# Attention probabilities transposed in 32x32 blocks and put in place by DMAs, instead of by TensorE

## The chip, the cores and the metric

The kernel runs on one core of a Trainium2 chip. The metric is the device time of one execution in microseconds; a kernel's time is the median of its runs.

## The reference

Two post-norm encoder layers over 512 tokens of width 1024, in float32. Each layer projects its input once for three kinds of attention: a (4 heads, dilated windows, written here as one dense softmax with an additive mask), b (8 query heads on 2 key heads, dense) and c (4 heads, a 2-D neighbourhood with a learned bias). Each is projected back to 1024, weighted by a sigmoid gate, and summed; then an output projection, a layer norm, a squared-ReLU MLP and another layer norm.

```
for layer in range(DEPTH):
    h = x @ w_in[layer]
    qa, ka, va, qb, kb, vb, qc, kc, vc, gate_logits = jnp.split(h, splits, axis=-1)
    ...
    merged = (g[:, :, 0] * (oa @ w_branch_a[layer])
              + g[:, :, 1] * (ob @ w_branch_b[layer])
              + g[:, :, 2] * (oc @ w_branch_c[layer]))
    mix = merged @ w_out[layer]
    x = layer_norm(DEEPNORM_ALPHA * x + mix, ln1_g[layer], ln1_b[layer])
    ff = jnp.square(jax.nn.relu(x @ w_up[layer])) @ w_down[layer]
    x = layer_norm(DEEPNORM_ALPHA * x + ff, ln2_g[layer], ln2_b[layer])
```

## The kernel before

Every large product is made of three matmuls: each operand is split into a high part (`whi`, `xTh`, `pth`; ScalarE rounds to fp32r) and a low part (`wlo`, `xTl`, `ptl`; VectorE subtracts), and hi x hi, lo x hi and hi x lo are summed in PSUM. Weights of 512 KB stream through two `raw` buffers (L194, issued by SyncE) and are split at L182 (ScalarE) and L183 (VectorE).

Attention goes over 64 slots a layer: heads a0 to a3, c0 to c3, b0 to b7, each in four blocks of 128 queries (`qb`). A slot's scores `pss` (two matmuls, L513 and L514) are made two slots ahead; then the maximum (L519 in b, L523 in a and c), its negative (L524), the exponential with its sum (L525), the reciprocal (L528) and the normalise (L529: GpSimd in a and b, VectorE in c). `turn` transposes p on TensorE, 128 keys at a time (L544, tile `psp`), and splits the result from PSUM into `pth` and `ptl`. When the head's four blocks are there, `values` multiplies them with the values (`pso`, L558 and L559, eight matmuls), one slot into the next head; ScalarE and VectorE bring the result together in `of` (L568, L569), and after each second head it is split into `oh` and `ol`.

Between the slots a queue of other work fills TensorE: projections, gates (`psg`, L585 is their tanh) and branch projections (`psb`, L607). `rate` says how many matmul triples of this filler go with each half of a slot. L617 is a GpSimd addition that merges a gated branch into `mg`. What each engine does stands in one fixed order of its own, which the compiler's scheduler chooses from the program's order. After the last head, `tail` computes the gates and branches of b, and the MLP follows.

## Time and profile before

| | before |
|---|---|
| median of 3 runs | 1547.91 us |
| lowest to highest | 1545.48 to 1548.38 us |
| the profiled execution | 1549.4 us |
| its span | 1547.6 us |
| TensorE busy (matmul) | 1527.6 us, 99% |
| VectorE busy | 866.0 us, 56% |
| ScalarE busy | 632.5 us, 41% |
| GpSimd busy | 182.0 us, 12% |

The span runs from the first to the last instruction of the profiled execution; 1.8 us of its own time lie around it. Shares are of the span, so they average over stages that differ.

### The profile page before, as it was taken

What the parts mean: (1) busy time and instruction counts of PE and PEld (TensorE: products, weight loads), DVE (VectorE), ACT (ScalarE), POOL (GpSimd) and SP (SyncE); (2) the same over time, 40 slices, a digit from 0 to 9 for tenths busy, and PEclk for the clock granted to TensorE, in tenths of its full rate; (3) what the DMA queues carried; (4) which work ended last, traced back from release to release, by engine and by line L of the source; (5) the groups of instructions that cost most, each with busy time, mean ns of one, the idle gap of its engine ahead of it and who ended that gap; (6) DMA issues with size and microseconds to landing.
All of it is one profiled execution on the core that took longest, in us unless ns stands there. A gap on an engine that the chain in (4) does not pass through costs nothing.

```text
span 1547.6 us, 19148 instructions
## 1 busy us (share of the span) xinstructions
PE 1527.6 (99%) x7400; PEld 1279.8 (83%) x7400; DVE 866.0 (56%) x1498; ACT 632.5 (41%) x1036; POOL 182.0 (12%) x190
## 2 busy tenths in 40 slices
PE   8999999999999999999999999999999999999997
PEld 6888888888898888888888888888888888888886
DVE  4678877644664314441566787776448542244315
ACT  4665666533144212431136556665332431134310
POOL 0113213211100000000102141233111000000001
PEclk9999999999999999999999999999999999999999
DMA  6222311153153323332331323112432432233311
GB/s 218 83 85 75 111 55 58 52 177 123 55 177 96 96 82 96 110 96 83 106 128 56 98 82 103 55 59 95 146 123 83 136 99 92 82 123 95 96 55 55
DMA packets 43434, 150.61 MB, mean 97 GB/s; under 512 B 5072, under 2 KB 5712, under 8 KB 43344
## 3 DMA queue, kind: packets, MB, share of 16 engines
q1 hardware_dynamic: 43344, 149.40, 30.5%
q8 instruction: 58, 0.95, 0.2%
q14 instruction: 32, 0.26, 0.1%
HBM read 145.19 MB, written 4.19 MB: 97 GB/s over the span
## 4 chain that ended last, share of the span: by engine, by line
PE 95%; DVE 2%; ACT 1%; DMA 1%; issue 0%; POOL 0%; SPq 0%; POOLq 0%; DVEq 0%; ACTq 0%
PE psd L155 9%; PE psd L154 9%; PE psd L153 9%; PE psu L154 8%; PE psu L155 8%; PE psu L153 8%; PE psg L155 6%; PE psg L154 6%; PE psg L153 6%; PE psp L544 3%; PE psq L155 2%; PE psq L153 2%; PE psq L154 2%; PE psb L155 2%; PE psb L153 2%; PE psb L154 2%
## 5 line engine op out<-in xcount | busy, mean ns | idle before, releaser
L183 DVE TENSOR_TENSOR wlo<-raw,whi 128x1024 fp32r<-128x1024 f32 (+1 forms) x246 | 306.9, 1248 | 421.5 <-ACT whi L182 420.5
L182 ACT ACTIVATE whi<-raw 128x1024 fp32r<-128x1024 f32 (+1 forms) x246 | 258.4, 1053 | 462.8 <-PE psd L155 143.1
L153 PE MATMUL psu<-xTh,whi 128*128 128x512 f32 (+1 forms) x576 | 210.8, 366 | 0.0
L154 PE MATMUL psu<-xTl,whi 128*128 128x512 f32 (+1 forms) x576 | 210.7, 366 | 0.0
L155 PE MATMUL psu<-xTh,wlo 128*128 128x512 f32 (+1 forms) x576 | 210.5, 365 | 0.0
L153 PE MATMUL psd<-whi,hh 128*128 128x512 f32 x512 | 199.3, 389 | 0.0
L155 PE MATMUL psd<-whi,hl 128*128 128x512 f32 x512 | 199.2, 389 | 0.0
L154 PE MATMUL psd<-wlo,hh 128*128 128x512 f32 x512 | 199.2, 389 | 0.0
L153 PE MATMUL psg<-xTh,whi 128*128 128x512 f32 x384 | 156.8, 408 | 0.0
L154 PE MATMUL psg<-xTl,whi 128*128 128x512 f32 x384 | 151.6, 395 | 0.0
L155 PE MATMUL psg<-xTh,wlo 128*128 128x512 f32 x384 | 151.6, 395 | 0.0
L154 PEld LDWEIGHTS psu<-xTl,whi 128*128 128x128 f32 x576 | 108.6, 189 | 17.7
L153 PEld LDWEIGHTS psu<-xTh,whi 128*128 128x128 f32 x576 | 108.6, 189 | 17.4
L155 PEld LDWEIGHTS psu<-xTh,wlo 128*128 128x128 f32 x576 | 108.6, 189 | 17.4
L266 POOL TENSOR_TENSOR ve<-ve,nhalf 128x1 f32<-128x1 f32 x16 | 24.2, 1513 | 775.0 <-DVE ve L265 775.0
L529 POOL TENSOR_SCALAR p<-p,stat 128x512 f32<-128x512 f32 x96 | 70.7, 737 | 360.2 <-DVE stat L528 242.9
L154 PEld LDWEIGHTS psd<-wlo,hh 128*128 128x128 f32 x512 | 96.1, 188 | 20.0
L153 PEld LDWEIGHTS psd<-whi,hh 128*128 128x128 f32 x512 | 96.1, 188 | 19.9
L155 PEld LDWEIGHTS psd<-whi,hl 128*128 128x128 f32 x512 | 96.1, 188 | 19.8
L153 PE MATMUL psq<-whi,xTh 128*128 128x512 f32 (+1 forms) x256 | 90.0, 351 | 7.2 <-ACT whi L182 6.7
L229 DVE TENSOR_TENSOR ptl<-psp,pth 128x512 fp32r<-128x512 f32 (+2 forms) x128 | 81.6, 637 | 21.2 <-ACT pth L228 19.8
L155 PE MATMUL psq<-whi,xTl 128*128 128x512 f32 (+1 forms) x256 | 87.9, 343 | 0.0
(116 smaller groups left out, 2572.7 us busy)
## 6 DMA issues: line engine op xcount, KB each, us to landing
raw<-in_w_up SPq DMA_DIRECT2D x64, 512.0 KB, 3.6
raw<-in_w_down SPq DMA_DIRECT2D x64, 512.0 KB, 3.5
raw<-in_w_gate SPq DMA_DIRECT2D x48, 512.0 KB, 3.5
raw<-in_w_qkv SPq DMA_DIRECT2D x22, 512.0 KB, 3.6
raw<-in_w_out SPq DMA_DIRECT2D x16, 512.0 KB, 3.6
raw<-in_w_c SPq DMA_DIRECT2D x12, 512.0 KB, 3.5
bias<-in_rpb SPq DMA_DIRECT2D x8, 640.0 KB, 3.9
raw<-in_w_bb SPq DMA_DIRECT2D x8, 512.0 KB, 3.6
```

Source lines behind the costliest of these rows:

```text
L153: nc.tensor.matmul(ps, lhs.hi, rhs.hi, start=start, stop=False)
L154: nc.tensor.matmul(ps, lhs.hi, rhs.lo, start=False, stop=False)
L155: nc.tensor.matmul(ps, lhs.lo, rhs.hi, start=False, stop=stop)
L182: nc.scalar.activation(hi[:, s], raw[:, s], AF.Copy)
L183: nc.vector.tensor_tensor(lo[:, s], raw[:, s], f32(hi[:, s]), op=ALU.subtract)
L229: nc.vector.tensor_tensor(dst.lo, ps, f32(dst.hi), op=ALU.subtract)
L266: nc.gpsimd.tensor_tensor(ve[:, 1:], ve[:, :1], nhalf[:, :1], op=ALU.pow)
L529: (nc.vector if name == "c" else nc.gpsimd).tensor_scalar(p, p, st[:, 3:4], 1.0, op0=ALU.mult, op1=ALU.mult)
L544: nc.tensor.transpose(ps[:, j * P:(j + 1) * P], p[:, j * P:(j + 1) * P], ident)
```

## The change

Each block of p is transposed by one VectorE instruction in 32x32 blocks (L552 of the new kernel) into `tx` (three buffers). When a head's four blocks are done, 16 DMAs of 32 rows by 2 KB (`gather`, L562; SyncE's queue, for the last head ScalarE's as well) put the blocks in place in `ptl` (two buffers). `settle` copies each quarter of it, rounded, to `pth`, which takes over the head's `tx` buffer (ScalarE, L577), and subtracts (GpSimd, L578). The values products of a head (L592) come two heads later instead of one. c's normalise moves from VectorE to GpSimd, and the blocks that c's neighbourhood never uses are zeroed by GpSimd. The maximum comes negated, so that L524 goes. `p` has three buffers instead of four, weights have 4 + 4 buffers instead of 5 + 3, the filler rates of c and b fall, and the tail makes half a gate ahead (`half_gate`).

```diff
-            pool, n = (extra[0], 3) if more else (wts, 5)
+            pool = extra[0] if more else wts
-            hi = pool.tile([P, 1024], F32R, tag="whi", name="whi", bufs=n)
-            lo = pool.tile([P, 1024], F32R, tag="wlo", name="wlo", bufs=n)
+            hi = pool.tile([P, 1024], F32R, tag="whi", name="whi", bufs=AHEAD)
+            lo = pool.tile([P, 1024], F32R, tag="wlo", name="wlo", bufs=AHEAD)
...
-            p = pool.tile([P, S], F32, tag="p", name="p", bufs=4)[:, :n]
+            p = pool.tile([P, S], F32, tag="p", name="p", bufs=3)[:, :n]
...
-                (nc.vector if name == "c" else nc.gpsimd).tensor_scalar(p, p, st[:, 3:4], 1.0, op0=ALU.mult, op1=ALU.mult)
+                nc.gpsimd.tensor_scalar(p, p, st[:, 3:4], 1.0, op0=ALU.mult, op1=ALU.mult)
...
-            ps = bank("psp")[:, :n * P]
-            for j in range(n):
-                nc.tensor.transpose(ps[:, j * P:(j + 1) * P], p[:, j * P:(j + 1) * P], ident)
-            split_psum(pt[:, k0:k1, qb * P:(qb + 1) * P], ps.rearrange("p (k q) -> p k q", q=P))
+            nc.vector.transpose(squares[name, h][1][:, :, k0:k1, qb].rearrange("p j k b -> p k j b"),
+                                p.rearrange("p (k j a) -> p k j a", j=4, a=SQ))
+
+        def gather(name, h, queues):
+
+            n, sq = squares[name, h]
+            lo = pool.tile([P, 4, TB, P], F32R, tag=f"ptl{n % 2}", name="ptl", bufs=1)
+            parts[name, h] = Split(None, lo)
+            for m in range(16):
+                i, j = m % 4, m // 4
+                queues[m % len(queues)].dma_start(f32(lo)[j * SQ:(j + 1) * SQ, i],
+                                                  sq[i * SQ:(i + 1) * SQ, j].rearrange("a k q b -> a k (q b)"))
...
+        def settle(name, h, kbs, engines=(nc.gpsimd, nc.gpsimd)):
+
+            pt = parts[name, h]
+            if pt.hi is None:
+                pt.hi = pool.tile([P, 4, TB, P], F32R, tag=f"tx{squares[name, h][0] % 3}", name="pth", bufs=1)
+            for kb in kbs:
+                q = keys_of(name, kb)
+                hi, lo = chosen(pt.hi[:, :, kb], *q), chosen(pt.lo[:, :, kb], *q)
+                nc.scalar.activation(hi, f32(lo), AF.Copy)
+                engines[kb % 2].tensor_tensor(lo, f32(lo), f32(hi), op=ALU.subtract)
...
-        rate = {"a": 2.1, "c": 2.85, "b": 1.6}
+        rate = {"a": 2.1, "c": 2.75, "b": 1.5}
...
-            if qb == 0 and i:
-                values(*slots[i - 1][:2])
-                if (name, h) == ("a", 2):
-                    flags.add("a")
             turn(name, h, qb, probs.popleft())
+            if qb == TB - 1:
+                gather(name, h, (nc.sync,) if i < len(slots) - 1 else (nc.sync, nc.scalar))
+                if i > TB:
+                    settle(*slots[i - TB][:2], (0, 1))
+            if qb in (0, 1) and i >= 2 * TB:
+                at = slots[i - 2 * TB][:2]
+                if qb == 0:
+                    settle(*at, (2, 3))
+                else:
+                    values(*at)
+                    if at == ("a", 1):
+                        flags.add("a")
...
         def tail():
-            steps = 0
+            a, b = slots[-1 - TB][:2], slots[-1][:2]
+            settle(*a, (2, 3))
+            ts = [drain(half_gate("b", 0))]
+            values(*a)
+            settle(*b, range(TB), (nc.vector, nc.gpsimd))
+            ts.append(drain(half_gate("b", 1)))
+            values(*b)
             for m in range(KB):
-                for _ in gated("b", m):
-                    steps += 1
-                    if steps == 4:
-                        values(*slots[-1][:2])
+                drain(gated("b", m, ts[m]))
+                if m + 2 < KB:
+                    ts.append(drain(half_gate("b", m + 2)))
                 yield merged[m]
```

The order of the instructions shows where this puts them. TensorE before, in the first layer, just ahead of the values products of head b1 (the next eight rows): psp_2418 is the last transposed block of b1, pss_2428 the scores of a later slot, psb_2437 six branch matmuls.

```order
L544 MATMUL psp_2418<-ident_73,p_2343 128x128 x4
L153 MATMUL psg_2369<-xTh_80,whi_2330 128x512
L154 MATMUL psg_2369<-xTl_81,whi_2330 128x512
L155 MATMUL psg_2369<-xTh_80,wlo_2331 128x512
L513 MATMUL pss_2428<-kh_1797,qs_2184 128x512
L514 MATMUL pss_2428<-kl_1798,qs_2184 128x512
L153 MATMUL psb_2437<-oh_1639,whi_2238 128x512
L154 MATMUL psb_2437<-ol_1640,whi_2238 128x512
L155 MATMUL psb_2437<-oh_1639,wlo_2239 128x512
L153 MATMUL psb_2437<-oh_2023,whi_2238 128x512
L154 MATMUL psb_2437<-ol_2024,whi_2238 128x512
L155 MATMUL psb_2437<-oh_2023,wlo_2239 128x512
```

TensorE of the change around the values products of head b1 (pso_2449): pss_2428 is now the last scores of head b3, psb_2442 six branch matmuls.

```order
L515 MATMUL pss_2428<-kh_1810,qs_2139 128x512
L516 MATMUL pss_2428<-kl_1811,qs_2139 128x512
L156 MATMUL psb_2442<-oh_1872,whi_2339 128x512
L157 MATMUL psb_2442<-ol_1873,whi_2339 128x512
L158 MATMUL psb_2442<-oh_1872,wlo_2340 128x512
L156 MATMUL psb_2442<-oh_2184,whi_2339 128x512
L157 MATMUL psb_2442<-ol_2185,whi_2339 128x512
L158 MATMUL psb_2442<-oh_2184,wlo_2340 128x512
L592 MATMUL pso_2449<-pth_2382,v_669 128x512
L592 MATMUL pso_2449<-ptl_2232,v_669 128x512
L592 MATMUL pso_2449<-pth_2382,v_669 128x512
L592 MATMUL pso_2449<-ptl_2232,v_669 128x512
```

The psp rows are gone, and the products of b1 (four of the eight shown) stand six matmuls behind the last scores of b3. GpSimd of the change at the same place: L532 is the normalise (p_2327, p_2355, p_2396 and p_2431 are the four blocks of b3, p_2431 made from pss_2428), ptl_2083 and ptl_2232 belong to b0 and b1, mg_487 is a merge.

```order
L578 TENSOR_TENSOR ptl_2083<-ptl_2083,pth_2249 128x4x128 x4
L532 TENSOR_SCALAR p_2327<-p_2327,stat_2328 128x512
L532 TENSOR_SCALAR p_2355<-p_2355,stat_2356 128x512
L532 TENSOR_SCALAR p_2396<-p_2396,stat_2397 128x512
L532 TENSOR_SCALAR p_2431<-p_2431,stat_2432 128x512
L661 TENSOR_TENSOR mg_487<-mg_487,t_2258 128x512
L578 TENSOR_TENSOR ptl_2232<-ptl_2232,pth_2382 128x4x128 x4
L532 TENSOR_SCALAR p_2483<-p_2483,stat_2484 128x512
```

GpSimd had only normalises and merges here; now a head's four subtractions stand together behind all four normalises of the head two later. ScalarE of the change at the start of the tail: t_3015 is the tanh of the second gate, pth_3044 and pth_3142 are the heads b6 and b7, whi_3092 the weights of the next gate.

```order
L231 ACTIVATE oh_2997<-of_2866 128x512
L562 DMA ptl_3027<-tx_2961 32x512 x6
L624 ACTIVATE t_3015<-psg_3016,hb_293 128x512
L577 ACTIVATE pth_3044<-ptl_2921 128x4x128 x4
L577 ACTIVATE pth_3142<-ptl_3027 128x4x128 x4
L185 ACTIVATE whi_3092<-raw_3088 128x1024
L185 ACTIVATE whi_3096<-raw_3090 128x1024
```

The eight pth copies stand ahead of the weights; on TensorE twelve branch matmuls follow the gate psg_3016, and then the gate that needs whi_3092.

## Rows read from the trace of the kernel before

**Rows 1.** The page: busy time by engine, and the granted clock in 40 slices.

```profile
PE 1527.6 (99%) x7400; PEld 1279.8 (83%) x7400; DVE 866.0 (56%) x1498; ACT 632.5 (41%) x1036; POOL 182.0 (12%) x190
...
PEclk9999999999999999999999999999999999999999
```

**Rows 2.** Busy time by window: five b heads, then the four c heads (layer one).

```profile
core 0: us, PE busy (x) PEld busy (x) DVE busy (x) ACT busy (x) POOL busy (x), PEclk, DMA share, GB/s
218.80:291.45 72.65, 72.65 (x361) 59.81 (x360) 53.47 (x108) 44.40 (x88) 22.87 (x26) 1.00 0.19 59
...
115.50:192.30 76.80, 76.80 (x383) 64.38 (x382) 64.46 (x158) 46.38 (x92) 21.87 (x21) 1.00 0.29 91
```

**Rows 3.** Groups by line and shape: TensorE's transposes (busy us, mean ns, idle before).

```profile
L544 PE MATMUL psp<-ident,p 128*128 128x128 f32 x464 | 72.0, 274 | 4.6 <-POOL p L529 4.6
```

**Rows 4.** Timeline of TensorE around one group of transposes (start us, us).

```profile
223.42 0.39 PE L155 MATMUL psg<-xTh,wlo 128*128 128x512 f32 x1
223.65 0.60 PE L544 MATMUL psp<-ident,p 128*128 128x128 f32 x4
224.00 0.48 PE L153 MATMUL psg<-xTh,whi 128*128 128x512 f32 x1
224.32 0.40 PE L154 MATMUL psg<-xTl,whi 128*128 128x512 f32 x1
```

**Rows 5.** Timeline of TensorE at the first transpose of layer one.

```profile
50.41 0.39 PE L153 MATMUL psg<-xTh,whi 128*128 128x512 f32 x1
53.08 0.66 PE L544 MATMUL psp<-ident,p 128*128 128x128 f32 x4 [2.28 <-POOL p L529]
```

**Rows 6.** Busy time by window, just behind the first transposes of layer one.

```profile
53.79:57.20 3.41, 3.41 (x9) 2.67 (x8) 1.64 (x5) 1.40 (x3) 0.57 (x1) 0.50 0.37 141
```

**Rows 7.** Groups by line and shape: the operations that the sum is made of.

```profile
L519 DVE TENSOR_REDUCE stat<-pss 128x1 f32<-128x512 f32 x64 | 43.8, 685 | 3.7 <-PE pss L514 3.3
L528 DVE RECIPROCAL stat<-stat 128x1 f32<-128x1 f32 x128 | 20.5, 160 | 44.8 <-ACT p L525 43.9
L229 DVE TENSOR_TENSOR ptl<-psp,pth 128x512 fp32r<-128x512 f32 x96 | 66.1, 689 | 20.4 <-ACT pth L228 19.5
L183 DVE TENSOR_TENSOR wlo<-raw,whi 128x1024 fp32r<-128x1024 f32 x242 | 304.2, 1257 | 420.3 <-ACT whi L182 419.3
L529 DVE TENSOR_SCALAR p<-p,stat 128x384 f32<-128x384 f32 x16 | 7.9, 491 | 0.2
...
L525 ACT ACTIVATE p<-pss,stat 128x512 f32<-128x512 f32 x64 | 44.0, 687 | 51.1 <-DVE stat L524 50.8
L525 ACT ACTIVATION_READ_ACCUMULATOR p<-pss,stat 128x1 f32 x64 | 12.4, 194 | 0.0
L228 ACT ACTIVATE hh<-r 128x512 fp32r<-128x512 f32 x64 | 40.4, 631 | 77.4 <-DVE r L844 77.4
L585 ACT ACTIVATE t<-psg,hb 128x512 f32<-128x512 f32 x32 | 21.7, 677 | 0.0
L182 ACT ACTIVATE whi<-raw 128x1024 fp32r<-128x1024 f32 x242 | 255.8, 1060 | 461.4 <-PE psd L155 143.1 <-DMA raw<-in_w_up 88.7 <-PE psu L154 87.6
...
L529 POOL TENSOR_SCALAR p<-p,stat 128x512 f32<-128x512 f32 x96 | 70.7, 737 | 360.2 <-DVE stat L528 242.9 <-DVE stat L524 90.9 <-PE pss L514 8.2
L617 POOL TENSOR_TENSOR mg<-mg,t 128x512 f32<-128x512 f32 x32 | 43.8, 1369 | 158.6 <-DVE t L607 158.6
```

**Rows 8.** Timelines of VectorE and GpSimd where they meet in SBUF.

```profile
345.49 2.35 DVE L183 TENSOR_TENSOR wlo<-raw,whi 128x1024 fp32r<-128x1024 f32 x1
...
345.46 1.29 POOL L617 TENSOR_TENSOR mg<-mg,t 128x512 f32<-128x512 f32 x1 [6.96 <-DVE t L607]
...
310.85 2.20 POOL L617 TENSOR_TENSOR mg<-mg,t 128x512 f32<-128x512 f32 x1 [4.23 <-DVE t L607]
```

**Rows 9.** SyncE's timeline (four issues), and the page's DMA issues (KB, us to landing).

```profile
1.64 1.85 SPq L194 DMA_DIRECT2D raw<-in_w_qkv  x4
...
raw<-in_w_gate SPq DMA_DIRECT2D x48, 512.0 KB, 3.5
```

More of the change, by code (lines that the diff above doesn't have):

```diff
@@ L29 @@
 RAWS = 2
+AHEAD = 4
+FIRST = [1, 1, 0, 0, 0, 0]
+SQ = 32
 NEG = -1e30
@@ L327, in project @@
                     yield cost
+                if tb == TB - 1:
+                    stream.free(w[i])
                 if i == nw - 1:
-                    if tb == TB - 1:
-                        for c in w:
-                            stream.free(c)
                     evac(tb, ps[tb])
@@ L418, in c_values @@
         def c_values(m):
-            while m == 0 and "a" not in flags:
+            while m == 0 and "a" not in flags or m == 1 and ("a", 1) not in oT:
                 yield None
@@ L536, in turn @@
             if qb == 0:
[L537 to L545 removed]
+                n = len(squares)
@@ L556, in values @@
                 q0, q1 = keys_of(name, kb)
-                sl = slice(q0 * P, q1 * P)
-                nc.tensor.matmul(po[:, sl], v[:, kb], pt.hi[:, kb, sl], start=i == 0, stop=False, skip_group_check=True)
-                nc.tensor.matmul(po[:, sl], v[:, kb], pt.lo[:, kb, sl], start=False, stop=i == TB - 1, skip_group_check=True)
+                to = chosen(po.rearrange("p (i r) -> p i r", i=4), q0, q1)
+                for n, part in enumerate((pt.hi, pt.lo)):
+                    nc.tensor.matmul(to, v[:, kb], chosen(part[:, :, kb], q0, q1), start=(i, n) == (0, 0),
+                                     stop=(i, n) == (TB - 1, 1), skip_group_check=True)
             half = (h % 2) * HD
@@ L565, in values @@
             if name == "c":
-                dst = by_columns(dst)
-                a, b = blocks(a), blocks(b)
-            nc.scalar.activation(dst, a, AF.Copy)
-            nc.vector.tensor_tensor(dst, dst, b, op=ALU.add)
+                to = dst.rearrange("p (i r q c) -> p i r q c", i=4, r=2, q=TB)
+                cut = [(lambda t, r=r: t.rearrange("p (i q r c) -> p i r q c", i=4, q=TB, r=2)[:, :, r], to[:, :, r])
+                       for r in range(2)]
+            else:
+                cut = [(lambda t: t.rearrange("p (i q b) -> p i q b", i=4, q=TB), dst.rearrange("p (q i b) -> p i q b", q=TB, i=4))]
+            for f, to in cut:
+                nc.scalar.activation(to, f(a), AF.Copy)
+                nc.vector.tensor_tensor(to, to, f(b), op=ALU.add)
             if half:
@@ L619, in branch_c @@
         def branch_c():
-            for m in range(KB):
-                yield from gated("c", m)
+            ts = []
+            for m in range(KB + 1):
+                if m < KB:
+                    ts.append((yield from half_gate("c", m)))
+                if m:
+                    while ("c", 1) not in oT:
+                        yield None
+                    yield from gated("c", m - 1, ts[m - 1])
         g = lambda br, ms: [w_gate[l, br * KB + m] for m in ms]
@@ L765, in encoder @@
     xp = right.enter_context(tc.tile_pool(name="x", bufs=1, side="right", reuse_waits="tile"))
-    stream.plan([w_qkv[0, i] for i in range(6)])
+    extra[0] = right.enter_context(tc.tile_pool(name="early", bufs=1, side="right", reuse_waits="tile"))
+    stream.plan([w_qkv[0, i] for i in range(6)], FIRST)
     def split_x(tb, t, cut):
```

57 lines of the change are left out of this document (37 added, 20 removed).

## Prediction

> **What bounds the kernel now.** I read the page's totals first. TensorE is busy 1527.6 of 1547.6 us, 99%, and its clock is at nine tenths or more in every slice [rows 1]; so what TensorE no longer does is gained, and what makes it wait is lost, one for one. Then the stretches: in a window of five b heads TensorE is busy for all 72.65 us, VectorE 53.47 (74%), ScalarE 44.40 (61%), GpSimd 22.87 (31%) [rows 2]. A b head takes 14.5 us there (72.65/5), and the other engines have slack. The reader should keep both shares in mind: the change gives TensorE less and GpSimd, the slowest engine for one operation, more. Last I read the one place in attention where TensorE already waits, the start of each layer's heads [rows 5, 6], since it shows what a wait does to the clock.
>
> All sums are made against the profiled execution's own 1549.4 us (span 1547.6 and 1.8 around it), 0.1% above the median of 1547.91. The three runs spread over 0.2%, so a difference under 0.2% (3 us) can't be told from none.
>
> **What goes.** The 464 transposes of p on TensorE go [rows 3]: 128 groups, 64 a layer (16 in a; 8 of three and 8 of two in c; 32 in b). Their busy time of 72.0 us is not their price, since matmuls overlap. The starts of neighbours show it: matmuls follow each other by 0.23 us (223.42 to 223.65), and from the start of the four transposes to the second matmul behind them 0.67 us pass (223.65 to 224.32) [rows 4], so a group of four costs 0.67 - 0.23 = 0.44 us, and in proportion three 0.33 and two 0.22. A layer has 48 x 0.44 + 8 x 0.33 + 8 x 0.22 = 25.5 us, both 51.0 us. In b the lower rate (1.5 for 1.6) also takes fillers out of the heads; the fillers left over (about 36 matmuls) run behind the last head, at no loss of their own.
>
> At the first transpose of a layer TensorE waits 2.28 us for p from GpSimd [rows 5], and the next 3.4 us run at a granted clock of 0.50, the 1.2 GHz level [rows 6]. No transpose stands there any more. I count 2.3 + 1.7 (half of 3.4) = 4 a layer, 8 us. Gains: 59 us, to 1490.4 if nothing else moved.
>
> **What is added off the path.** VectorE: 128 block transposes in place of 128 subtractions ptl of 0.69 us. The trace has no such operation. Below, the normalise of 384 elements at 0.49 gives 0.65 for 512 by size, and if it were twice as quick per element 0.33; above, the subtraction of twice the size takes 1.257 [rows 7]. I take 0.69, as nearly all VectorE rows of 512 elements do, so the swap is free; VectorE had 26% idle. ScalarE: pth is read from SBUF instead of PSUM, 0.631 by the row of hh, which reads SBUF too. SyncE: 16 transfers a head, 0.46 us of issue each (1.85/4), 7.4 us, and a 512 KB load lands 3.5 us after issue [rows 9]; some 11 us after the last transpose of head h all should be there, while settling starts only behind the last normalise of head h+2, two head times (over 25 us) on. That gap hides them. Weight loads queue behind these issues on SyncE; they are hidden by the four split weights ahead. Without that cover each head would pay several us. The 4 + 4 weight buffers hold as many weights as 5 + 3 and I count them at nothing. The four c heads take 76.80 us, with GpSimd busy 21.87 [rows 2]; the change adds at most 4 x (4 x 0.74 + 4 x 1.37) = 34 us of normalising and settling there, 56 of 77, and the values products come two heads later with over 20 matmuls in between: I count c at nothing.
>
> **What is added on the path.** Settling puts four subtractions (L578) per head on GpSimd, and the order fixes where: behind the last normalise of head h+2, with the values products of h right behind that head's last scores on TensorE. So in a b head this chain has to run between the last pss and the end of pso: reduce 0.685, exp 0.687 + 0.194, reciprocal 0.160, normalise 0.737, together 2.46; then four subtractions. GpSimd's price for one: below, the normalise (0.74); above, the same kind of operation held up by VectorE (2.20 [rows 8]); I take the L617 row, 1.369, the same operation on the same size [rows 7]. Four make 5.48, the chain 7.94 us, and in b1 a merge (L617) stands in front of them, 1.37 more. What TensorE has to do meanwhile, counted in the order, the products themselves included: 23, 14, 32, 26, 23 and 14 matmuls for b0 to b5 (b1's 14 are shown in the order above), 132, at 0.229 us 30.2 us a layer. The six chains take 6 x 7.94 + 1.37 = 49.0 us, and each is longer than its cover (b2's by 0.6, b1's by 6.1). So TensorE waits at least 18.8 us a layer, **37.6 us** in both.
>
> In the tail (b6, b7) ScalarE's order, shown above, puts eight pth copies ahead of whi for the next gate. From the end of the gate before: tanh 0.677, eight copies of 0.631, whi 1.060, wlo 1.257 make 8.0 us; TensorE has twelve branch matmuls and two of the gate to do, 3.2 us. It waits 4.8 us a layer, **9.6 us**.
>
> The sum of what the order forces: 1549.4 - 51.0 - 8 + 37.6 + 9.6 = 1537.6 us.
>
> **What comes on top.** Three things, none of which the order shows.
> Lock: in the trace wlo takes 2.35 instead of 1.257 where it starts 0.03 us behind a GpSimd subtraction, and a GpSimd one takes 2.20 where it meets VectorE [rows 8]. The new place of whi is right behind the four pth copies, so its wlo falls among the four subtractions in six heads a layer: about 1 us each, 12 us.
> The Trainium skill ("SBUF — State Buffer", section "Who interferes with whom") says that a VectorE instruction with two SBUF inputs and a GpSimd instruction that reads SBUF exclude each other: the second waits for all of the first. By it these 12 us come at every meeting. By the L617 group alone, whose mean of 1.369 is near the 1.29 of one undisturbed, they would be nothing and the sum 1560.
> Queues: reduce, exp, reciprocal and pth are four steps whose engines are 74% and 61% busy in that window; half an operation's wait (about 0.35 us) at such shares is 0.2 to 0.25 each, 1 us a chain, 12 us.
> Clock: a wait of 2.28 us was followed by 3.4 us at half speed, 1.7 lost. Four of six chains (b0, b1, b4, b5) and the tail leave more than 2.3 us of waiting, ten places in all, at most 17 us; the waits are cut up, as pso takes its blocks one by one, and part of the slow time falls into the next wait. I take 10.
> Together 34: **1572 us**, 1.5% slower.
>
> **The rivals.**
> R1, the other side: only the forced chain counts, the three extras are hidden. For it: GpSimd has nothing else to do in the waits, and VectorE idles 26%. Against it: the lengthened rows [rows 8] and the half clock [rows 6]. It gives 1538, and is the truth (faster) wherever the extras stay under 8 us, that is under 0.7 us a chain.
> R2: the change does what it says, because GpSimd's subtraction costs no more than its normalise, 0.74. The chain is then 5.4 us, longer than its cover in b1 (3.6) and b5 (2.2) and hardly in b0 and b4 (0.15): 6 us a layer. 1490.4 + 12 + 9.6 = 1512. Against it: L617 at 1.369 and 32 times.
> R3: the block transpose costs as much as 1.25 us. VectorE's work of a head grows by 2.2 us, the reduce that heads the chain queues behind it, and I count 2 us more in each of twelve chains and the full 17 for the clock: 1572 + 24 + 7 = 1603, up to 1612.
> R4: the gathered blocks land after the settling wants them. Two head times hide 11 us, so each of the 16 would have to take longer than one 512 KB load; little speaks for it. Each us beyond that cover would come in all 32 heads: 1538 + 34 + 32 = 1604 for one.
>
> **How the numbers follow.** Forecast 0.55 (1550 to 1600: extras from 12 to 62 us), R1 0.22, R2 0.10, R3 0.11, R4 0.02. The predicted time is the forecast's, 1572. R2's 1512 and R3's 1612 are the ends of the range; below and above lie half of R2 and some of R3 and R4, under 2 in 10. Faster by over 0.2%: R2 and most of R1 (extras under 8 us), 0.30; within 0.2%: the seam of R1 and the forecast, 0.05; slower: the rest, 0.65.
>
> **What would show it.** No psp rows, and TensorE's instructions fewer by 464. In the windows of b, TensorE's busy share falls well under 100% and its idle time stands before pso, released by GpSimd's ptl (L578); the groups show that at 1.3 to 1.5 us and 128 of them. A b head takes 16 to 18 us instead of 14.5. Stretches of PEclk 0.50 follow the longest waits. At the start of attention the 2.28 us wait is gone. In the tail TensorE waits for whi or wlo about 5 us. Wrong would be: L578 near 0.75 us (R2); waits before pso released by ScalarE's pth or a DMA (R4); STREAM_TRANSPOSE over 1 us (R3); or GpSimd starting a head's subtractions before its normalises, so that the chain isn't in series at all.

## The result, and the profile after

The changed kernel takes 1637.07 us (median; 1635.28 to 1638.37) against 1547.84 us in the same comparison: ratio 1.058, 95% interval 1.056 to 1.060. It is slower, as forecast, but by 89 us and not by 24, outside the range of 1512 to 1612. The profiled execution took 1636.45 us (span 1634.1), 87.05 more than that of before.

The page of the changed kernel: busy time by engine, and the granted clock.

```profile
PE 1537.6 (94%) x6936; PEld 1255.6 (77%) x6936; DVE 863.7 (53%) x1350; ACT 632.7 (39%) x1044; POOL 374.8 (23%) x378
...
PEclk9998999889999999999999989887999999999999
```

Against [rows 1], 464 fewer instructions on TensorE, GpSimd's time doubled, and a clock that drops in the attention of both layers. TensorE's busy time rose although it has less to do: at half clock the same matmul lasts longer. The loss by the clock is (1 - granted clock) x time: mean clocks of 0.996 and 0.962 make 6 us before and 62 after, of which 3 and 2 us lie behind TensorE's last matmul and cost nothing.

The stages show where. Each window runs from the last scores of one kind of head to the last of the next: c, then b, then the tail to the first matmul of the MLP. The windows of the kernel before, first layer (columns as in [rows 2]):

```profile
107.31:182.96 75.65, 75.65 (x381) 63.59 (x379) 63.88 (x157) 45.54 (x90) 22.68 (x22) 1.00 0.31 96
182.96:303.15 120.19, 120.19 (x597) 99.11 (x595) 88.59 (x181) 72.22 (x143) 31.22 (x38) 1.00 0.20 58
303.15:422.74 119.59, 119.59 (x539) 98.56 (x538) 62.24 (x78) 38.75 (x51) 18.42 (x14) 1.00 0.36 118
```

The windows of the changed kernel, both layers:

```profile
93.08:180.58 87.50, 76.28 (x327) 60.77 (x326) 59.39 (x128) 43.78 (x89) 56.75 (x69) 0.94 0.48 134
180.58:320.67 140.09, 118.05 (x454) 87.81 (x453) 89.09 (x154) 72.33 (x147) 70.11 (x70) 0.90 0.42 108
320.67:465.28 144.61, 136.43 (x570) 108.97 (x569) 74.27 (x87) 51.57 (x68) 39.42 (x26) 0.94 0.41 127
901.62:991.67 90.05, 77.82 (x328) 62.05 (x326) 63.07 (x134) 48.38 (x98) 56.87 (x73) 0.92 0.45 126
991.67:1129.34 137.67, 120.97 (x454) 89.83 (x453) 87.07 (x148) 67.98 (x139) 66.68 (x65) 0.86 0.40 109
1129.34:1274.57 145.23, 134.66 (x570) 107.66 (x569) 76.30 (x87) 51.62 (x68) 36.42 (x26) 0.95 0.40 126
```

In each row, length less PE busy is TensorE's waiting, and (1 - PEclk) x length the clock's loss. Both layers together, in us:

| stage | waits | clock | forecast of waits | forecast of clock |
|---|---|---|---|---|
| c | 23.4 | 12.5 | 0 | 0 |
| b | 38.7 | 33.3 | 61.6 (chains, lock, queues) | 10 |
| tail | 18.8 | 16.0 | 9.6 | (in the 10) |

1549.4 - 59 + 80.9 + 61.8 = 1633.1, 3 us short of the measured 1636.45. That it comes out so close is in part luck. The clocks in the rows have two digits; the 19 stretches at 0.50 in these windows add up to 119.5 us, a loss of 60 and not 62. And TensorE waits for 19.5 of these 119.5 us, so that some 10 us stand in both columns. A cost that no column has may stand in place of these 12 us: a matmul lasts 0.39 us and the next starts 0.23 us behind it, so each wait ends an overlap of 0.16 us, and for 63 more waits that is 10 us, an estimate. (b5's chain ends behind the last scores, so about 8 us of the tail's waits are b's.) The MLP is as before: behind the second layer's attention 359.53 us in both kernels. The new operations, by group:

```profile
L578 POOL TENSOR_TENSOR ptl<-ptl,pth 128x512 fp32r<-128x512 f32 x92 | 135.9, 1505 | 7.7 <-ACT pth L577 7.1 <-DMA raw<-in_w_c 0.2 <-DMA ptl<-tx 0.2
...
L552 DVE STREAM_TRANSPOSE tx<-p 128x512 f32<-128x512 f32 x96 | 68.0, 708 | 34.8 <-POOL p L532 32.1 <-DMA ptl<-tx 1.8
L577 ACT ACTIVATE pth<-ptl 128x512 fp32r<-128x512 f32 x96 | 52.8, 619 | 1.8 <-DMA ptl<-tx 1.8
```

The block transpose takes 0.708 us (0.69 taken), the copy 0.619 (0.631), GpSimd's subtraction 1.505 (1.369 alone, 1.3 to 1.5 with the lock). None of these prices explains 65 us. What TensorE waited for, all waits of the execution (us, times, longest):

```profile
PE pso L592 <- POOL ptl L578: 31.2, 37, 2.9
PE pso L592 <- ACT pth L577: 13.6, 10, 2.0
PE psg L156 <- ACT whi L185: 12.3, 4, 5.5
PE psq L156 <- ACT whi L185: 11.4, 4, 6.7
PE psg L158 <- DVE wlo L186: 6.8, 5, 2.7
PE psc L158 <- DVE wlo L186: 4.7, 2, 2.9
PE psq L157 <- DVE wlo L186: 3.5, 3, 1.6
PE psc L156 <- ACT whi L185: 3.5, 1, 3.5
```

44.8 us before pso, as foreseen in kind (42.1 of them in b and behind it, 2.7 in c); but 42.2 us for weights, of which 6.7 stand at the start of the program (as before) and 10.8 in the two tails: the other 24.7, 20.5 of them in the windows of c and 4.2 in b, were not foreseen at all.

Head b1 of the first layer shows the chain. TensorE's timeline from b3's last scores into the products of b1:

```profile
248.24 0.39 PE L516 MATMUL pss<-kl,qs 128*128 128x512 f32 x1
...
249.63 0.40 PE L158 MATMUL psb<-oh,wlo 128*128 128x512 f32 x1
250.80 0.50 PE L592 MATMUL pso<-pth,v 128*128 128x512 f32 x1 [0.77 <-ACT pth L577]
254.21 0.79 PE L592 MATMUL pso<-ptl,v 128*128 128x512 f32 x1 [2.91 <-POOL ptl L578]
254.81 0.63 PE L592 MATMUL pso<-pth,v 128*128 128x512 f32 x1
256.42 0.80 PE L592 MATMUL pso<-ptl,v 128*128 128x512 f32 x1 [0.98 <-POOL ptl L578]
```

GpSimd's timeline beside it:

```profile
250.96 0.69 POOL L532 TENSOR_SCALAR p<-p,stat 128x512 f32<-128x512 f32 x1 [1.86 <-DVE stat L531]
251.67 1.27 POOL L661 TENSOR_TENSOR mg<-mg,t 128x512 f32<-128x512 f32 x1
252.90 5.93 POOL L578 TENSOR_TENSOR ptl<-ptl,pth 128x512 fp32r<-128x512 f32 x4
```

And a window of the changed kernel, from the last 0.35 us of the wait of 2.91 us on:

```profile
253.86:260.69 6.83, 5.47 (x10) 3.01 (x11) 1.74 (x2) 0.95 (x2) 4.97 (x4) 0.50 0.26 77
```

Normalise, merge, four subtractions, in that order: from the last scores (248.24) to the end of the fourth subtraction (252.90 + 5.93 = 258.83) 10.6 us, where 7.94 + 1.37 = 9.3 were reckoned. And the clock falls to 0.50 (1.2 GHz) for 6.83 us at the end of the waits of 0.77 and 2.91 us. The matmuls in the rows above last 0.63 to 0.80 us there for 0.39. Part of the slow time covers what would have been waiting; in b1 TensorE waits 4.7 us where the chain of 10.6 us less its cover of 3.2 (an estimate: 14 matmuls at 0.229) would have left 7.4.

### The profile page after: what moved, and what is told of

Read it like the earlier page. It is cut to its first block, busy times and chain, and to the rows that moved or that the text cites. A ratio compares the mean times of both kernels' runs of the same rounds, so it can differ in the third digit from the quotient of the medians.

```text
span 1634.1 us, 19188 instructions
## 1 busy us (share of the span) xinstructions
PE 1537.6 (94%) x6936; PEld 1255.6 (77%) x6936; DVE 863.7 (53%) x1350; ACT 632.7 (39%) x1044; POOL 374.8 (23%) x378
## 4 chain that ended last, share of the span: by engine, by line
PE 71%; POOL 9%; DVE 6%; DMA 5%; SPq 4%; issue 3%; ACT 2%; POOLq 0%; ACTq 0%; DVEq 0%
PE psd L156 9%; PE psd L158 9%; PE psd L157 9%; PE psu L157 7%; PE psu L156 7%; PE psu L158 7%; POOL ptl L578 6%; PE psg L158 4%; PE psg L156 4%; PE psg L157 3%; SPq L562 3%; DMA ptl<-tx 3%; PE pso L592 2%; DVE wlo L186 2%; POOL p L532 2%
## 5 line engine op out<-in xcount | busy, mean ns | idle before, releaser
L186 DVE TENSOR_TENSOR wlo<-raw,whi 128x1024 fp32r<-128x1024 f32 (+1 forms) x246 | 318.4, 1296 | 432.0 <-ACT whi L185 431.3
L578 POOL TENSOR_TENSOR ptl<-ptl,pth 128x512 fp32r<-128x512 f32 (+2 forms) x124 | 169.2, 1393 | 8.5 <-ACT pth L577 7.1
L156 PE MATMUL psg<-xTh,whi 128*128 128x512 f32 x384 | 156.2, 407 | 12.4 <-ACT whi L185 12.3
L532 POOL TENSOR_SCALAR p<-p,stat 128x512 f32<-128x512 f32 (+2 forms) x128 | 91.9, 719 | 316.6 <-DVE stat L531 307.7
L156 PEld LDWEIGHTS psu<-xTh,whi 128*128 128x128 f32 x576 | 108.6, 189 | 17.5
L158 PEld LDWEIGHTS psu<-xTh,wlo 128*128 128x128 f32 x576 | 108.6, 189 | 17.5
L552 DVE STREAM_TRANSPOSE tx<-p 128x512 f32<-128x512 f32 (+2 forms) x128 | 84.3, 659 | 53.9 <-POOL p L532 50.4
```

The source lines that it names most:

```text
L156: nc.tensor.matmul(ps, lhs.hi, rhs.hi, start=start, stop=False)
L158: nc.tensor.matmul(ps, lhs.lo, rhs.hi, start=False, stop=stop)
L186: nc.vector.tensor_tensor(lo[:, s], raw[:, s], f32(hi[:, s]), op=ALU.subtract)
L532: nc.gpsimd.tensor_scalar(p, p, st[:, 3:4], 1.0, op0=ALU.mult, op1=ALU.mult)
L552: nc.vector.transpose(squares[name, h][1][:, :, k0:k1, qb].rearrange("p j k b -> p k j b"), p.rearrange("p (k j a) -> p k j a", j=4, a=SQ))
L578: engines[kb % 2].tensor_tensor(lo, f32(lo), f32(hi), op=ALU.subtract)
```

## The experiments

All times are medians. The changed kernel is 1637.07 us; ratios are against the kernel before. Each run's clock loss is worked out from its mean clock and span, as above. In the edits, "..." stands for lines left out.

**e1, GpSimd in the program's order.**

```diff
-        for i, (name, h, qb) in enumerate(slots):
...
+        with tc.manual_schedule(engines={mybir.EngineType.Pool}):
+            for i, (name, h, qb) in enumerate(slots):
...
```

> The changed kernel with GpSimd's instructions of the 64 slots in the order in which the program writes them, so that a head's four subtractions stand in two pairs between the normalises of the head two later, and not all four behind its last one. Nothing else is changed. Theory S (the series chain last scores - normalise - four subtractions - values sets TensorE's waits in b): TensorE's waits before pso fall from 44.8 us to under 20, the granted clock's loss in b falls with them, and the time goes to about 1595 us (1575 to 1610). Rival A (it is the amount of work on GpSimd, or its meetings with VectorE, not the place): within 8 us of 1637. Rival Q (weights and gathers queue on SyncE, and that is most of the loss): within 8 us of 1637 too, with the waits before pso gone but others longer.

1638.47 us, ratio 1.058 (1.057 to 1.060). No gain, a miss for theory S; waits before pso grew to 70 us. That is rival A's number, but the trace shows another reason: on ScalarE the four copies still stand behind the last exponential, and GpSimd's first pair now blocks its normalises until they come. ScalarE's timeline in e1, and under it GpSimd's:

```profile
268.57 2.18 ACT L577 ACTIVATE pth<-ptl 128x512 fp32r<-128x512 f32 x4
```

```profile
269.27 2.55 POOL L578 TENSOR_TENSOR ptl<-ptl,pth 128x512 fp32r<-128x512 f32 x2 [7.75 <-DMA ptl<-tx]
```

GpSimd idles 7.75 us until the first copy is done (the row names a DMA, but the copy of 268.57 ends 0.1 us before). Both engines have to be reordered, as e5 and e9 do.

**e2, every other subtraction on VectorE.**

```diff
-        def settle(name, h, kbs, engines=(nc.gpsimd, nc.gpsimd)):
+        def settle(name, h, kbs, engines=(nc.vector, nc.gpsimd)):
```

> The changed kernel with the subtractions of every other quarter (L578) on VectorE instead of GpSimd, two of four per head, with no order imposed. Theory S: the serial part of the chain behind the last normalise is 2 x 1.4 us on GpSimd beside 2 x 0.69 on VectorE instead of 4 x 1.4, the waits before pso fall by 2 to 3 us a head in the twelve heads, and the half clock behind them goes with them: about 1590 us (1570 to 1610). Rival A (amount of work on GpSimd): about the same gain, since GpSimd is relieved by 90 us. Rival Q (the queue on SyncE): 1630 or more.

1584.53 us, ratio 1.024 (1.022 to 1.026), as theory S and rival A both had it, so that it does not part them: waits before pso 28 us, clock loss 30 us instead of 62.

**e3, filler in the waits.**

```diff
+            warm = bank("warm") if name == "b" and h < 6 else None
...
+                    if name == "b" and h < 6 and (n == 1 or i == 0):
+                        for _ in range(3):
+                            nc.tensor.matmul(warm, xT.hi[:, 0, 0], xT.hi[:, 0, 0:4], start=True, stop=True)
```

> The changed kernel with 15 more matmuls of 512 columns (3.4 us at full clock) per head b0 to b5 ahead of and between its values products, into a PSUM bank that nothing reads; the result is unchanged. They stand where TensorE waited 3 to 4 us a head. Theory C (the half clock behind the waits costs about 36 us in b, more than the waits themselves): the waits are filled, the clock stays up, and in spite of 180 matmuls more (41 us of work) the time falls to about 1612 us (1600 to 1625), the clock's loss in the trace from 63 us to under 35. Rival W (the waits cost only their own length): no change to 1637, or slower by up to 20 where a wait is shorter than the filler.

1654.58 us, 17.5 slower; a miss for theory C's number, and inside what rival W allowed (up to 20). The scheduler put nearly all of the filler ahead of the first product (13 of 15 matmuls in b1), where the wait was short, and 35 us of waits before pso were left. The clock loss fell by 22 us, to 40. Inconclusive, so e10.

**e4, weight loads on ScalarE's queue.** A `stream.queue` that is `nc.scalar` during the slots:

```diff
-nc.sync.dma_start(raw[:, s], src[:, s])
+self.queue.dma_start(raw[:, s], src[:, s])
```

> The changed kernel with the weight loads of the 64 slots issued from ScalarE's queue instead of SyncE's, so that they no longer stand behind the 16 gathers of a head, nor the gathers behind their waits. Theory Q (the queue on SyncE makes weights and blocks late in a and c): TensorE's waits for whi and wlo in psq, psc and psg fall from 25 us to under 10 with the half clock behind them, and the time to about 1605 us (1590 to 1620). Rival O (whi and wlo are late because they stand behind other work in the orders of ScalarE and VectorE, whose transposes wait for GpSimd): within 8 us of 1637, or slower, since ScalarE gets 0.33 to 0.5 us more per load.

1588.71 us, ratio 1.026 (1.024 to 1.028): quicker than theory Q had it, and not for its reason. The order moved too (the matmuls between the last scores and the end of pso in b went from 23, 14, 32, 26, 23, 14 to 11, 13, 17, 21, 23, 17, with subtractions between normalises), and most of the gain lies in b: 120.1 and 122.2 us for 140.1 and 137.7. Waits for whi and wlo, without the start, were 31 us for 35.5; mostly their places changed.

**e5, ScalarE and GpSimd in the program's order.** As e1, with `mybir.EngineType.Activation` in the set.

> As e1, but with ScalarE's instructions of the slots in the program's order too: in e1 the pth copies still stood behind the last exponential of head h+2 on ScalarE, so GpSimd's pairs waited for them. Here each pair of copies and each pair of subtractions stands between the exponentials and normalises, half a head to a head earlier. Theory S (the chain in series sets the waits in b, and the half clock follows them): waits before pso fall from 45 us to under 15, the clock's loss from 63 to under 35, the time to about 1575 us (1555 to 1595). Rival A (the amount of work on GpSimd and its meetings with VectorE): 1620 or more, with GpSimd's subtractions still released last. Rival Q (SyncE's queue): waits before pso then end on the gathers, 1610 or more.

1623.02 us, ratio 1.048 (1.047 to 1.050). b gains in theory S's direction (waits before pso 23 us, where S wanted under 15; stage 121.0 and 119.6 us), but in a and c ScalarE's fixed order puts whi behind copies and exponentials that wait: c's stage grew from 87.5 to 97.1 us. The time missed S's range (1555 to 1595), so e9 separates the two.

**e6, one transfer a head.**

```diff
-            for m in range(16):
-                i, j = m % 4, m // 4
-                queues[m % len(queues)].dma_start(f32(lo)[j * SQ:(j + 1) * SQ, i],
-                                                  sq[i * SQ:(i + 1) * SQ, j].rearrange("a k q b -> a k (q b)"))
+            queues[0].dma_start(f32(lo), sq.rearrange("p j k q b -> p j k (q b)"))
```

> The changed kernel with one DMA of the whole tile per head (1 MB, 8 KB a row) instead of 16, with the same bytes, but the blocks are not put in place: the 32x32 blocks stay where VectorE left them, so the values products multiply the wrong blocks. SyncE's issue falls from 10 us a head to under 1, and the scheduler, which reckons with fewer transfers, places settling earlier too (11 matmuls between the last scores and the end of pso in every b head). Theory Q (SyncE's queue makes weights late in a and c, and the reckoned transfers make settling late in b): waits for whi and wlo in a and c from 25 us to under 10, waits before pso under 15, about 1560 us (1535 to 1585). Rival V (VectorE, ScalarE and GpSimd in series are too slow whatever the queue): 1600 or more.

This version leaves the placing out: the 32x32 blocks stay where VectorE left them, so its products are of the wrong blocks, and only its time is of use. 1559.87 us, ratio 1.007 (1.005 to 1.009). b takes 114 us, 6 less than in the kernel before, with the same compute operations on every engine. What went are the 16 issues, whose row in the changed kernel (SyncE) is

```profile
239.95 10.01 SPq L562 DMA_DIRECT2D ptl<-tx  x16
```

0.63 us each, where 0.46 was taken; and with them the late place that the scheduler gave to settling: eleven matmuls now stand from the last scores to the end of pso in every b head. In the trace of the changed kernel b1's blocks were issued by 237.4 us and take 2.0 us to land, 11 us before their copies start at 250.13: the transfers were not late, the order was. c takes 82.5 and 82.7 us, against 87.5 and 90.0 in the changed kernel and 75.65 before. So about half of c's loss goes with the transfers, and half stays without them. Whether that half went by the queue or by the order, e6 does not tell.

**e7, four weights in the kernel before.**

```diff
-            pool, n = (extra[0], 3) if more else (wts, 5)
+            pool, n = (extra[0], 3) if more else (wts, 4)
...
-                if self.used[more] == (5, 3)[more]:
+                if self.used[more] == (4, 3)[more]:
```

> The kernel before with 4 buffers instead of 5 for split weights outside the MLP's extra 3 (so 4 in attention, as in the changed kernel). Theory Q (weights are late in the changed kernel for the queue): 0 to 4 us slower than before. Rival B (one buffer less is what makes weights late): 12 us or more slower, with waits for whi and wlo in psq and psc as in the changed kernel (about 25 us).

1560.85 us, ratio 1.008 (1.006 to 1.009): by its total, rival B's number. By stages it is not: the first MLP starts 0.8 us later (423.5 for 422.7) and the second layer's attention (from a's last scores) takes 2.2 us more, with no waits for whi in attention; the rest, some 9 us, is in the MLP, which here has seven buffers, while the change gives it eight. One buffer less in attention costs the kernel before 3 us. What a fifth would give the changed kernel was not run.

**e8, e2 and e4 together.**

> e2 and e4 together: every other subtraction on VectorE and the weight loads of the slots on ScalarE's queue. If the two act on different waits (b's chain, and the weights), gains add up to about 100 us of the 89 to be had: 1545 us (1530 to 1560). If they act on the same waits: 1575 to 1590.

1567.39 us, ratio 1.012 (1.011 to 1.014), between the two ranges: the gains of 52 and 48 us overlap in part, together they make 70.

**e9, the program's order in b only.** The region of e5 opened at the first slot of b.

> As e5, but with ScalarE's and GpSimd's instructions in the program's order only in the slots of b; a and c keep the scheduler's order. Theory S (the place of settling in b makes b's waits; a and c are another matter): the stretch from c3's to b5's values products falls from 111.7 us to about 92, as in e5, and a and c stay at 219.7 us; in both layers 40 us less, about 1597 us (1585 to 1608). Rival (e5's gain was not in b's order but in fewer half-clock stretches by chance): above 1615.

1593.89 us, ratio 1.030 (1.028 to 1.031), theory S's number. From c3's to b5's values products 93.0 and 91.2 us, where it was 111.7 and 114.4; waits before pso 15 us. GpSimd at b's slots now:

```profile
256.14 1.37 POOL L532 TENSOR_SCALAR p<-p,stat 128x512 f32<-128x512 f32 x2 [5.16 <-DVE stat L531]
257.48 2.55 POOL L578 TENSOR_TENSOR ptl<-ptl,pth 128x512 fp32r<-128x512 f32 x2
261.68 0.69 POOL L532 TENSOR_SCALAR p<-p,stat 128x512 f32<-128x512 f32 x1 [1.64 <-DVE stat L531]
```

The same work on the same engine, in pairs between the normalises, is 43 us cheaper: about half of the 89 us lost is the place of settling in b, and not its amount.

**e10, filler between the products.** e3 with TensorE's order fixed inside the products:

```diff
+                with tc.manual_schedule(engines={mybir.EngineType.PE}) if name == "b" and h < 6 else nullcontext():
...
+                        if name == "b" and h < 6 and n == 1:
+                            for _ in range((8, 4, 2, 2)[i]):
+                                nc.tensor.matmul(warm, xT.hi[:, 0, 0], xT.hi[:, 0, 0:4], start=True, stop=True)
...
```

> As e3, but the order on TensorE within the values products of b0 to b5 is fixed: 8, 4, 2 and 2 matmuls that nothing reads stand between the first product of a quarter (which needs pth) and the second (which needs ptl), where the waits of 2.9 and 1.0 us were; 192 matmuls, 44 us at full clock. Theory C (the half clock behind the waits is a large price of its own): the clock's loss in the trace falls from 63 us to under 35 and the time stays within 15 us of 1637 in spite of the 44 us. Rival W (a wait costs its own length, and the clock is down for another reason): the loss stays near 60 and the time grows by 20 us or more.

1625.13 us: 12 us faster with 44 us more work. The window of b, first layer:

```profile
179.67:318.28 138.61, 126.36 (x534) 98.96 (x533) 88.62 (x154) 73.22 (x149) 66.99 (x70) 0.98 0.42 110
```

80 matmuls more than in the changed kernel (534 for 454), waits of 12.3 us for 22.0, and a clock of 0.98 for 0.90. Over the execution the clock loss fell from 62 to 31 us, and TensorE's waits in the six windows of attention by 25. That is theory C's number, but it does not isolate the clock, since settling moved as well. In b1 the last scores start at 246.47, and GpSimd begins the subtractions 2.2 us later, ahead of the merge:

```profile
248.66 3.81 POOL L578 TENSOR_TENSOR ptl<-ptl,pth 128x512 fp32r<-128x512 f32 x3 [1.57 <-DMA ptl<-tx]
```

In the changed kernel it was 4.7 us later. The products of four of the six heads end 1 to 4 us sooner behind the last scores. So filled waits go with a higher clock, here and in e3; how much of the 12 us is the clock and how much the earlier place stays open. That slow matmuls cost time is seen directly, in b1's rows (0.63 us for 0.39).

**e11, gathers on two queues.** `(nc.sync, nc.scalar)` for every head.

> The changed kernel with the 16 gathers of every head issued half by SyncE and half by ScalarE (as the last head's already are). Theory Q (16 issues of 0.63 us on one queue hold up weights and settling): about 1600 us (1580 to 1615), with fewer waits for whi and wlo in a and c and an earlier place of settling. Rival O (the in-order queues of ScalarE and VectorE make the weights late): ScalarE's 5 us more a head make it 1637 or slower.

1600.40 us, ratio 1.034 (1.031 to 1.036), theory Q's number, but c grew to 91.7 and 90.0 us and waits before pso to 52 us. The gain is in b and the tail, whose orders moved again. But the waits for whi and wlo, without the start, fell from 35.5 to 12 us (in c from 20.5 to 3.4), as theory Q wanted, so the gathers on SyncE's queue do bear on the weights. What c saved there came back before pso, 21.6 us in c's windows.

**e12, e9 with e2 and e4.**

> e9, e2 and e4 together: b in the program's order on ScalarE and GpSimd, every other subtraction on VectorE, and the slots' weight loads on ScalarE's queue. If b's order, GpSimd's share and the queue are separate losses: b as in e9 with 5 us less, a and c as in e8 (207.7 us at c3): about 1550 us (1535 to 1565), with a chance of being under the kernel before. If they overlap: 1565 to 1580, no better than e8.

1591.97 us, ratio 1.029 (1.027 to 1.031): a miss, worse than e8. With e4's order b had already its pairs between normalises; fixing ScalarE's order there only put whi behind them (waits of psg for whi and wlo 24 us).

**e13, c's GpSimd work on VectorE.**

```diff
-nc.gpsimd.tensor_scalar(p, p, st[:, 3:4], 1.0, op0=ALU.mult, op1=ALU.mult)
+(nc.vector if name == "c" else nc.gpsimd).tensor_scalar(p, p, st[:, 3:4], 1.0, op0=ALU.mult, op1=ALU.mult)
...
-engines[kb % 2].tensor_tensor(lo, f32(lo), f32(hi), op=ALU.subtract)
+(nc.vector if name == "c" else engines[kb % 2]).tensor_tensor(lo, f32(lo), f32(hi), op=ALU.subtract)
```

> The changed kernel with c's normalise back on VectorE and c's subtractions (L578) on VectorE too; a and b as in the change. Theory O (in c, weights are late because whi and wlo stand in the in-order queues of ScalarE and VectorE behind transposes and rope steps that wait for GpSimd, which got c's normalise and settling): the stretch from a's last scores to c's last falls from 87.5 and 90.0 us to about 79, about 1610 us (1595 to 1622). Rival K (four weight buffers, held by b's projection, or SyncE's queue): the stretch stays at 86 or more, 1630 to 1640.

1620.67 us, ratio 1.047 (1.046 to 1.049). c's stage fell to 85.6 and 82.3 us, by 1.9 and 7.7, half of what theory O wanted; b's fell by 3.9 and 2.8. GpSimd's share in c is a part of it; the waits of psc (9.0 us) stayed.

**e14, the tail's weights listed early.** The two `stream.plan` lines of the tail moved ahead of the slots.

> The changed kernel with the list of the tail's weights made before the 64 slots instead of behind them, so that their loads are issued ahead of the last gathers and their whi stand between b6's and b7's pth copies on ScalarE, not behind all eight. Theory S (the eight copies ahead of whi make the tail's wait, with half clock behind it): TensorE's waits of 3.6 and 5.5 us for whi in the tail are gone, and the stretch from the last scores to the MLP falls from 144.6 to about 135, about 1618 us (1610 to 1626). Rival (the tail waits for settling itself, b6's and b7's): a wait before pso takes its place, 1630 or more.

1623.78 us, ratio 1.049 (1.048 to 1.051), 13 us gained; the tail 139.1 and 139.0 us for 144.6 and 145.2, a little less than expected. The wait it removes, on ScalarE and TensorE of the changed kernel:

```profile
341.02 4.40 ACT L577 ACTIVATE pth<-ptl 128x512 fp32r<-128x512 f32 x8
345.64 1.06 ACT L185 ACTIVATE whi<-raw 128x1024 fp32r<-128x1024 f32 x1 [0.22 <-DMA raw<-in_w_gate]
```

```profile
346.75 0.79 PE L156 MATMUL psg<-xTh,whi 128*128 128x512 f32 x1 [3.61 <-ACT whi L185]
```

The copies end at 345.42, but whi starts at 345.64, when its weights land. SyncE's timeline shows why they land so late: the load stands behind 24 gathers of b6 and b7, which hold the queue for 28 us (in 7.6 of them it waits for b5's products).

```profile
313.55 28.09 SPq L562 DMA_DIRECT2D ptl<-tx  x24
341.74 1.03 SPq L197 DMA_DIRECT2D raw<-in_w_gate  x2
```

Two paths end within 0.22 us of each other (0.34 us in the second layer): the eight copies on ScalarE, and the load behind the gathers. Without the copies the wait would have been as long. e14 moves whi on both queues, so it removes the wait and does not tell the two apart; no run does.

**e15, e8 with e14.**

> e8 (every other subtraction on VectorE, the slots' weight loads on ScalarE's queue) with the tail's weights early as in e14. If the tail's loss is apart from the others: 1567 less 20, about 1547 us (1538 to 1556), level with the kernel before. If the waits only move: 1560 or more.

1547.26 us, ratio 0.9995 (0.9986 to 1.0004): level with the kernel before. One large wait is left, twice 8 us of psc for whi.

**e16, e15 with c's normalise on VectorE.**

> e15 with c's normalise back on VectorE as well. Theory O: c's stretch falls by another 2 to 4 us a layer, about 1541 us (1530 to 1550), under the kernel before. If c's waits are not GpSimd's: as e15.

1549.32 us, ratio 1.0004 (0.9996 to 1.0013): c fell by 0.9 and 2.2 us, and b gave it back (4.5 us in the second layer).

**e17 and e18, b's query projection frees its weights earlier.**

```diff
-        bq = project(512, b_q, 1)
+        bq = project(512, b_q, 1, order=[(tb, i) for t in (0, 2) for i in range(4) for tb in (t, t + 1)])
```

> e15 with b's query projection going over the four weights for token blocks 0 and 1, then for 2 and 3, so that its first weight is free 36 matmuls before its end and not 18, and the next whi stands ahead of oh on ScalarE. Theory K (four buffers held to the projection's end, and whi behind oh, make the 8 us wait in psc): the wait is gone or under 2 us, the half clock behind it too, and the time falls by 2 x (8 + 4) to about 1523 us (1515 to 1533), under the kernel before. Rival: the wait only moves to the next gate, 1540 or more.

e18 has `[(tb, i) for i in range(4) for tb in range(4)]`.

> e15 with the projection going over each weight for all four token blocks (four PSUM banks held), so that weights are freed one by one through it. Theory K: as e17, within 5 us, or a little slower since four of eight PSUM banks are held and the four blocks' rope steps come together at the end: 1520 to 1540 us. Rival: the banks make scores wait, above 1545.

1549.00 us, ratio 1.0007 (0.9998 to 1.0015), and 1546.14 us, ratio 0.9989 (0.9980 to 0.9998). Both miss theory K's times (1523, and 1520 to 1540). The wait in psc is gone in both, and it came back elsewhere, as e17's rival said. In e18 c's windows take 74.7 and 69.5 us (82.2 and 80.1 in e15), and b's 121.4 and 123.2 (114.7 and 112.8). TensorE's waits in e17 (us, times, longest):

```profile
PE psk L439 <- DVE rw L398: 18.6, 4, 5.1
```

TensorE's transposes of b's rotated queries wait for the rope steps. In the changed kernel these steps hold up whi, and GpSimd's new work stands ahead of them. The second layer shows it, on GpSimd and then on VectorE:

```profile
938.27 5.04 POOL L578 TENSOR_TENSOR ptl<-ptl,pth 128x512 fp32r<-128x512 f32 x4
943.30 0.58 POOL L532 TENSOR_SCALAR p<-p,stat 128x384 f32<-128x384 f32 x1
943.85 2.44 POOL L391 TENSOR_TENSOR t<-rw,cs 128x256 f32<-128x256 f32 x4
```

```profile
943.91 0.58 DVE L552 STREAM_TRANSPOSE tx<-p 128x384 f32<-128x384 f32 x1 [3.53 <-POOL p L532]
945.30 0.80 DVE L395 TENSOR_TENSOR rw<-rw,cs 128x512 f32<-128x512 f32 x1 [0.81 <-POOL t L391]
...
953.05 0.69 DVE L608 TENSOR_TENSOR of<-of,pso 64x512 f32<-64x512 f32 x1
```

ScalarE and TensorE behind them:

```profile
953.77 0.63 ACT L231 ACTIVATE oh<-of 128x512 fp32r<-128x512 f32 x1 [3.57 <-DVE of L608]
954.31 1.04 ACT L185 ACTIVATE whi<-raw 128x1024 fp32r<-128x1024 f32 x1
```

```profile
955.40 0.50 PE L156 MATMUL psc<-xTh,whi 128*128 128x512 f32 x1 [3.50 <-ACT whi L185]
```

Four subtractions of 5.04 us (of an a head, which e13 leaves on GpSimd) stand ahead of a normalise and of a rope product on GpSimd, and VectorE waits 3.53 us for that normalise. `of` is queued behind the rope steps, `oh` waits for `of`, whi stands behind `oh`, and TensorE waits 3.50 us for whi. How much earlier whi would come without the subtractions these rows do not show. A step of the rope that did not get slower is GpSimd's power (L382, 1.97 us; 1.97 to 3.40 in the kernel before). e18 is the quickest version, 0.1% under the kernel before, less than what a measurement of this kernel can tell.

## Why the prediction was right and wrong

**What goes.** Right as far as shown: the first transposes' wait and its half clock are gone (a's window has no waiting), and the MLP's time did not move.

**Prices off the path.** VectorE's 0.708 and ScalarE's 0.619 were right, so R3 is out. SyncE's issue was mis-sized, 0.63 us and not 0.46. "Weight loads queue behind these issues on SyncE; they are hidden by the four split weights ahead" failed: in the tail the next gate's weights are issued behind 28 us of gathers and land when TensorE already waits, and with the gathers on two queues (e11) the waits for weights fell by 23 us. What the queue costs by itself stays open, since every run that eased it moved the order as well (e4, e6, e11).

**The chain in b.** Right in mechanism, place and nearly in size: 42.1 us before pso in b and behind it, against 37.6 forced. e9 shows it: with the same operations in another place the waits before pso are 15 us. The additions for lock and queues (24 us) were too much by some 20. The lengthened operations are there (subtractions at 1.505, wlo in the b1 chain 1.96 for 1.257); that the slow matmuls cut the waits short is seen in b1 and argued for the rest.

**The tail.** Right in size, 10.8 us for whi and wlo against 9.6 forecast, and half by luck. The eight copies are there, but the load behind the gathers on SyncE ends the wait, 0.22 and 0.34 us later, and the prediction had counted that queue as hidden.

**"I count c at nothing."** This step failed: 23.4 us of waits and 12 of clock. I compared GpSimd's sum of work (56 of 77 us; it was 56.75 of 87.5) with the stage, where what counts is the order in which the engines wait for one another. The rows under e17 show one such chain: GpSimd's new subtractions delay a normalise and the rope steps, these hold up VectorE's queue, and whi is queued behind (3.50 us). All waits of c for whi and wlo are 20.5 us. With half of the subtractions off GpSimd c's windows are 15 us shorter in both layers together (e2, 82.1 and 80.3 us), with c's own work off it 9.6 us (e13), without the transfers 12 us (e6). They overlap, and each moved the order; the exact shares are open.

**"Clock: I take 10."** This step failed most: 60 us, 48 of them in b and the tail, which the 10 were for. I had one pattern, 2.28 us of waiting and 3.4 us at half speed [rows 5, 6], and took 10 of at most 17 because waits are cut up. The trace shows the opposite: 19 stretches in attention, 3.4 to 10.2 us long, and with cut-up waits (0.77, then 2.91, then 0.98 in b1) the clock stayed at 0.50 for 6.83 us. Fillers in the waits took 22 us (e3) and 31 us (e10) off the loss; how much of that was a gain in time no run isolates. The Trainium skill ("TensorE: Matmul & The Clock Gate", section "HAM oscillation — how this bites in real kernels") describes a kernel whose matmuls come in bursts with waits for DMAs between them: the clock drops again after each wait, and half of the time spent at the low clock is lost. The rows here agree as to the half (behind b1's products, from 259.47 us on, two matmuls follow each other by 0.43 us for 0.23), though the waits are for engines; not every wait here was followed by a drop: the execution has 67 waits and 19 stretches.

Of the rivals, R1 and R2 are out (subtractions at 1.505, waits where the chain said). R4 is out in b, where b1's blocks had landed 11 us before they were wanted; only in the second tail did copies wait for blocks, 1.77 us. That the transfers still cost so much came by a way that no rival had: the scheduler settles late where it has 16 transfers to place, and early with one (e6). In sum the forecast was 65 us short: 35 by c, 38 by the clock in b and the tail, less 14 that the waits of b and the tail stayed under theirs; some 5 are left.

## What to carry to other kernels

Price a wait of TensorE with the half clock behind it, above all where short waits follow each other: here 81 us of waits came with 60 us of clock. A sum of work per engine does not show whether in-order queues fit; follow for each moved operation which engine's queue it blocks, and who is behind (e1, e9, e17). When a change goes wrong on the order, reorder before giving up operations: the same instructions cost 43 us less in another place, and with three repairs (e15) the change is level with the kernel before.

## What was not expected of the hardware

Sixteen gathers of 64 KB take 10.01 us of SyncE's queue, 0.63 us each, against 0.46 for a load of the same queue in [rows 9]; they land 2.0 us after issue (median). A VectorE operation on 10 elements a partition (L381) took 1.08 us where GpSimd finished L391 and then zeroed tx beside it (143.99 us; it ended when the zeroing did), and 0.17 at 138.56. In e6 the same line took 0.91 us beside a GpSimd subtraction that ended with it (150.28 us). These are two meetings; no run here isolates them.
